# Add and gelu over 1024 x 4096 floats: another formula for the gelu, x in two loads, five adds moved to VectorE, another wait for the first store

## The chip, the cores and the metric

One core of a Trainium2 chip. The metric is the device time of one execution in microseconds (us), the median over runs of the same chip. A "span" is the time from the first to the last instruction in a profile, 1.4 to 1.7 us less than the device time. A ratio of two kernels is the mean time of one kernel's fast runs over the mean of the other's fast runs in the same rounds, so it is not quite the ratio of the medians quoted beside it.

## The reference

```python
x, y: 1024 x 4096 float32
z = x + y
out = 0.5 * z * (1 + tanh(sqrt(2/pi) * (z + 0.044715 * z**3)))
```

Each of the 128 partitions (rows of the on-chip memory) holds 32,768 elements (128 KB) of z. 33.55 MB come in, 16.78 MB go out.

## The kernel before

All transfers are issued by SyncE, an engine that computes nothing here, on one queue; VectorE, ScalarE and GpSimd compute. x, y and z lie in the on-chip memory SBUF, the tiles w in a second one, PSUM. z takes the place of x (one 128 KB row per partition); y goes through two buffers of 8192 columns, so y2 and y3 wait until y0 and y1 have been added. The columns are computed in 16 chunks of 2048, with two PSUM tiles w.

```python
loads = [8192, 8192, 8192, 8192]     # x and y, alternating: x0 y0 x1 y1 ...
FIRST = 9
stores = [16384, 10240, 6144]        # chunks 0-7, 8-12, 13-15
by_pool = set(range(1, C))           # adds on GpSimd: all but chunk 0
...
add(c):  z = z + y                                  # GpSimd (chunk 0: VectorE)
sq(c):   w = Square(root * z)                       # ScalarE, SBUF -> PSUM
stt(c):  w = (w + c1) * z                           # VectorE
sig(c):  w = Sigmoid(w)                             # ScalarE
mul(c):  z = w * z                                  # VectorE; chunk FIRST in two halves
...
store(0) also waits for the first half of mul(FIRST):
    reason="the stores join the queue when the last load is nearly done"
```

The moment at which the first store is issued is called the **join** below.

## Time and profile before

| | before |
|---|---|
| device time, median of 3 | 120.51 us (120.43 to 120.77) |
| span of the profiled run | 118.7 us |
| DMA engines busy | 98.8% of the span |
| VectorE / ScalarE / GpSimd busy | 73.7 / 61.0 / 69.6 us |
| first compute / join / last store issued | 21.85 / 77.34 / 106.77 us |

No compute engine is near full and the DMA engines are, so the reader should ask of each instruction only whether a transfer waits for it. The lines that carry this are shown in the prediction. One view adds to them, the longest entries of what SyncE's queue waited for (columns: who waited, for whom, us in total, times, longest):

```profile
SPq L139 <- DVE z L175: 46.2, 3, 17.8
SPq L135 <- POOL z L152: 31.4, 2, 18.1
SPq L135 <- DVE z L152: 21.6, 1, 21.6
```

SyncE waits most of the time for VectorE (stores) and GpSimd (y buffers). That looks like a bound by compute, but is not: while SyncE waits, the queue still holds transfers that it issued before.

### The profile page before, as it was taken

Reading aid. Unit: us, or ns where it says so; the run is one execution under the profiler, and the core shown is the slowest. Engines: PE = TensorE matmul, PEld = TensorE weight load, DVE = VectorE, ACT = ScalarE, POOL = GpSimd, SP = SyncE. Lnnn points to the kernel's source line nnn. Section 1 sums busy time; section 2 is a strip of 40 time slices with the busy share of each in tenths; the row PEclk is TensorE's granted clock in tenths of the full one; section 3 lists DMA queues with packets and bytes.
Section 4 is the critical chain, followed back from the end, with each engine's and each line's share of the span. In section 5 each row is a group of like instructions: output and inputs, shape, how many; then the busy total and the mean of one; then the engine's idle time right before and its main releaser. Section 6 shows DMA issues by size and latency. Waiting matters only on the chain.

```text
span 118.7 us, 172 instructions
## 1 busy us (share of the span) xinstructions
DVE 73.7 (62%) x35; ACT 61.0 (51%) x34; POOL 69.6 (59%) x19
## 2 busy tenths in 40 slices
DVE  0000000635799995739999968999994999990000
ACT  5000000063888965197698647888839779810000
POOL 0000000699996099999959999959999990000000
DMA  8989898989999898989999898998899889999896
GB/s 254 453 364 519 353 530 353 497 386 453 431 409 475 364 519 353 530 353 475 409 409 475 364 519 353 530 530 353 353 508 552 353 353 442 442 442 442 381 414 265
DMA packets 1584, 50.33 MB, mean 424 GB/s; under 512 B 176, under 2 KB 176, under 8 KB 176
## 3 DMA queue, kind: packets, MB, share of 16 engines
q1 hardware_dynamic: 1584, 50.33, 98.8%
HBM read 33.55 MB, written 16.78 MB: 424 GB/s over the span
## 4 chain that ended last, share of the span: by engine, by line
DMA 51%; POOL 26%; POOLq 4%; DVE 4%; DVEq 2%; ACT 2%; issue 0%; SPq 0%
DMA y<-in_y_dram 51%; POOL z L152 26%; POOLq L230 4%; DVE w L163 2%; DVEq L230 2%; DVE z L175 2%; ACT w L157 2%; SPq L128 0%; POOLq L152 0%
## 5 line engine op out<-in xcount | busy, mean ns | idle before, releaser
L152 POOL TENSOR_TENSOR z<-z,y 128x2048 f32<-128x2048 f32 x15 | 69.4, 4659 | 28.2 <-DMA y<-in_y_dram 28.2
L157 ACT ACTIVATE w<-z 128x2048 f32<-128x2048 f32 x16 | 30.1, 1882 | 37.6 <-DVE z L152 21.4
L163 DVE SCALAR_TENSOR_TENSOR w<-w,z 128x2048 f32<-128x2048 f32 x16 | 36.7, 2296 | 11.2 <-ACT w L157 11.0
L175 DVE TENSOR_TENSOR z<-w,z 128x2048 f32<-128x2048 f32 (+1 forms) x17 | 35.9, 2155 | 0.0
L168 ACT ACTIVATE w<-w 128x2048 f32<-128x2048 f32 x16 | 29.7, 1855 | 4.4 <-DVE w L163 4.3
L152 DVE TENSOR_TENSOR z<-z,y 128x2048 f32<-128x2048 f32 x1 | 2.3, 2293 | 20.5 <-DMA y<-in_y_dram 20.5
L215 ACT ACT_TABLE_LOAD x1 | 1.3, 1283 | 1.3 <-PEq L247 1.3
L214 DVE MEMSET one<- 128x1 f32 x1 | 0.1, 59 | 1.3 <-PEq L247 1.3
L247 POOL MEMSET const-float32-0.0<- 128x1 f32 x1 | 0.1, 99 | 0.2 <-issue 0.2
L215 ACT ACTIVATE one<-one 128x1 f32<-128x1 f32 x1 | 0.2, 203 | 0.0
L247 POOL MEMSET const-bfloat16-1.0<- 128x1 bf16 x1 | 0.1, 102 | 0.0
L247 POOL MEMSET const-uint8-127<- 128x1 uint8 x1 | 0.1, 102 | 0.0
L247 POOL MEMSET const-float32-1.0<- 128x1 f32 x1 | 0.1, 99 | 0.0
## 6 DMA issues: line engine op xcount, KB each, us to landing
z<-in_x_dram SPq DMA_DIRECT2D x4, 4096.0 KB, 31.3
y<-in_y_dram SPq DMA_DIRECT2D x4, 4096.0 KB, 22.2
out_dram<-z SPq DMA_DIRECT2D x1, 5120.0 KB, 15.8
out_dram<-z SPq DMA_DIRECT2D x1, 3072.0 KB, 11.9
out_dram<-z SPq DMA_DIRECT2D x1, 22.0
```

Source lines behind the costliest of these rows:

```text
L152: eng.tensor_add(out=zt[:, a:b], in0=zt[:, a:b], in1=yt[s][:, o : o + b - a])
L157: nc.scalar.activation(out=wt[c], in_=zt[:, a:b], func=act.Square, scale=root)
L163: nc.vector.scalar_tensor_tensor(out=wt[c], in0=wt[c], scalar=c1, in1=zt[:, a:b], op0=alu.add, op1=alu.mult)
L168: nc.scalar.activation(out=wt[c], in_=wt[c], func=act.Sigmoid)
L175: ins = nc.vector.tensor_mul(out=zt[:, a + o : a + o + n], in0=wt[c][:, o : o + n], in1=zt[:, a + o : a + o + n],)
L214: nc.vector.memset(one, 0.0)
L215: nc.scalar.activation(out=one, in_=one, func=act.Sigmoid)
L230: tc.compile()
L247: nc = _bacc.Bacc("TRN2", target_bir_lowering=False, num_devices=1)
```

## The change

The intent: gelu(z) = max(z, 0) + gelu(-|z|) needs one VectorE operation per chunk instead of two; VectorE can then take some of the adds from GpSimd; x in rows of 64 KB halves its packets.

```diff
-    loads = [8192, 8192, 8192, 8192]
-    FIRST = 9
+    xloads = [16384, 16384]
+    yloads = [8192, 8192, 8192, 8192]     # order: x0 y0 y1 x1 y2 y3
+    FIRST = 8
-    by_pool = set(range(1, C))
+    by_dve = {0: 0, 2: 0, 4: 2, 6: 4, 8: 8, 12: 10}   # add k on VectorE, ahead of end(by_dve[k])
...
-    sq:   w = Square(root * z)
-    stt:  w = (w + c1) * z
-    sig:  w = Sigmoid(w)
-    mul:  z = w * z
+    mag:  w = Abs(z)                          # ScalarE
+    gelu: w = Gelu_apprx_tanh(-1.0 * w)       # ScalarE
+    end:  z = max(z, 0) + w                   # VectorE, scalar_tensor_tensor
```

(The order on ScalarE becomes mag, gelu of one chunk after another, and the table loaded at the start is the gelu's.)

More of the change, by code (lines that the diff above doesn't have):

```diff
@@ L1 @@
 from contextlib import ExitStack
-import math
 import concourse.bass as bass
@@ L93 @@
     xv, yv, ov = (a.rearrange("(p n) d -> p (n d)", p=P) for a in (x, y, out))
-    c1 = 2.0 * math.sqrt(2.0 / math.pi)
-    root = math.sqrt(c1 * 0.044715)
     YS = 8192
@@ L108, in ranges @@
         return [(e - f, e) for e, f in zip(ends, sizes)]
-    lr, sr, cr = ranges(loads), ranges(stores), ranges([CH] * (TOT // CH))
+    xr, yr, sr, cr = (ranges(r) for r in (xloads, yloads, stores, [CH] * (TOT // CH)))
     C = len(cr)
-    by_pool = set(range(1, C))
+    by_dve = {0: 0, 2: 0, 4: 2, 6: 4, 8: 8, 12: 10}
     def over(rs, lo, hi):
@@ L123 @@
     zt = pool_sb.tile([P, TOT], fp32, tag="z", name="z")
-    yt, wt, muls = {}, {}, {}
+    yt, wt, ends = {}, {}, {}
     def load_x(i):
-        a, b = lr[i]
+        a, b = xr[i]
         nc.sync.dma_start(out=zt[:, a:b], in_=xv[:, a:b])
     def load_y(i):
-        a, b = lr[i]
+        a, b = yr[i]
         s, o = divmod(a, YS)
@@ L142, in store @@
                 ins.ins,
-                muls[FIRST].name,
+                ends[FIRST].name,
                 mybir.DependencyInfo(mybir.DependencyClass.Sync, mybir.DependencyReason.DATA),
@@ L150, in add, with mag, gelu, end @@
         s, o = divmod(a, YS)
-        eng = nc.gpsimd if c in by_pool else nc.vector
+        eng = nc.vector if c in by_dve else nc.gpsimd
         eng.tensor_add(out=zt[:, a:b], in0=zt[:, a:b], in1=yt[s][:, o : o + b - a])
-    def sq(c):
+    def mag(c):
         a, b = cr[c]
         wt[c] = pool_w.tile([P, CH], fp32, tag="w", name=f"w{c}")
+        nc.scalar.activation(out=wt[c], in_=zt[:, a:b], func=act.Abs)
+    def gelu(c):
         nc.scalar.activation(
-            out=wt[c], in_=zt[:, a:b], func=act.Square, scale=root
+            out=wt[c], in_=wt[c], func=act.Gelu_apprx_tanh, scale=-1.0
         )
-    def stt(c):
-        a, b = cr[c]
-        nc.vector.scalar_tensor_tensor(
-            out=wt[c], in0=wt[c], scalar=c1, in1=zt[:, a:b], op0=alu.add, op1=alu.mult
-        )
-    def sig(c):
-        nc.scalar.activation(out=wt[c], in_=wt[c], func=act.Sigmoid)
-    def mul(c):
+    def end(c):
         a, b = cr[c]
@@ L174, in mul @@
         for o in range(0, b - a, n):
-            ins = nc.vector.tensor_mul(
-                out=zt[:, a + o : a + o + n],
-                in0=wt[c][:, o : o + n],
-                in1=zt[:, a + o : a + o + n],
+            ins = nc.vector.scalar_tensor_tensor(
+                out=zt[:, a + o : a + o + n], in0=zt[:, a + o : a + o + n], scalar=0.0,
+                in1=wt[c][:, o : o + n], op0=alu.max, op1=alu.add,
             )
-            muls.setdefault(c, ins.ins)
+            ends.setdefault(c, ins.ins)
     sp = []
-    for i in range(len(loads)):
-        sp += [(load_x, i), (load_y, i)]
+    for i, (a, b) in enumerate(xr):
+        sp += [(load_x, i)] + [(load_y, j) for j, (c, _) in enumerate(yr) if a <= c < b]
     sp += [(store, i) for i in range(len(stores))]
-    pool = [(add, c) for c in range(C) if c in by_pool]
-    dve = [(add, c) for c in range(C) if c not in by_pool]
-    acts = [(sq, 0), (sq, 1)]
-    for c in range(0, C, 2):
-        dve += [(stt, c), (stt, c + 1), (mul, c), (mul, c + 1)]
-        acts += [(sig, c), (sig, c + 1)]
-        if c + 2 < C:
-            acts += [(sq, c + 2), (sq, c + 3)]
+    pool = [(add, c) for c in range(C) if c not in by_dve]
+    dve, acts = [], []
+    for c in range(C):
+        dve += [(add, k) for k in sorted(by_dve) if by_dve[k] == c] + [(end, c)]
+        acts += [(mag, c), (gelu, c)]
     needs = {
@@ L198 @@
         load_y: lambda i: [
-            (add, c)
-            for c in over(cr, lr[i][0] - 2 * YS, lr[i][0] - YS)
-            if lr[i][0] % YS == 0
-        ],
-        add: lambda c: [(f, i) for i in over(lr, *cr[c]) for f in (load_x, load_y)],
-        sq: lambda c: [(add, c)] + ([(mul, c - PS)] if c >= PS else []),
-        stt: lambda c: [(sq, c)],
-        sig: lambda c: [(stt, c)],
-        mul: lambda c: [(sig, c)],
-        store: lambda i: [(mul, c) for c in over(cr, *sr[i])] + [(mul, FIRST)],
+            (add, c) for c in over(cr, yr[i][0] - 2 * YS, yr[i][1] - 2 * YS)
+        ],
+        add: lambda c: [(load_x, i) for i in over(xr, *cr[c])]
+        + [(load_y, i) for i in over(yr, *cr[c])],
+        mag: lambda c: [(add, c)] + ([(end, c - PS)] if c >= PS else []),
+        gelu: lambda c: [(mag, c)],
+        end: lambda c: [(gelu, c)],
+        store: lambda i: [(end, c) for c in over(cr, *sr[i])] + [(end, FIRST)],
     }
@@ L214 @@
         nc.vector.memset(one, 0.0)
-        nc.scalar.activation(out=one, in_=one, func=act.Sigmoid)
+        nc.scalar.activation(out=one, in_=one, func=act.Gelu_apprx_tanh)
         while any(queues):
```

## The prediction

> **What bounds the kernel now.** I read the page first, then the timeline, the waits of the DMA queue, and the DMA view cut into stretches of 0.2 us. The page's queue and issue lines:
>
> ```profile
> span 118.7 us, 172 instructions
> q1 hardware_dynamic: 1584, 50.33, 98.8%
> HBM read 33.55 MB, written 16.78 MB: 424 GB/s over the span
> L152 POOL TENSOR_TENSOR z<-z,y 128x2048 f32<-128x2048 f32 x15 | 69.4, 4659 | 28.2 <-DMA y<-in_y_dram 28.2
> L157 ACT ACTIVATE w<-z 128x2048 f32<-128x2048 f32 x16 | 30.1, 1882 | 37.6 <-DVE z L152 21.4
> L175 DVE TENSOR_TENSOR z<-w,z 128x2048 f32<-128x2048 f32 (+1 forms) x17 | 35.9, 2155 | 0.0
> ```
>
> The 16 DMA engines are busy 98.8% of the span; no compute engine passes 62%. In the timeline GpSimd's first adds of the four y tiles start at 21.89, 41.31, 60.74 and 80.15: every 8.39 MB takes 19.4 us, 433 GB/s. Issue plus time to landing puts the stores' ends at 99.3 (77.34 + 22.0), 111.5 (95.66 + 15.8) and 118.7 (106.77 + 11.9), so the 8.39, 5.24 and 3.15 MB of stores run at 432 to 437 GB/s. One stream of 50.33 MB at 433 GB/s is 116.2 us; with some 2.4 us before the first and after the last byte it is the whole span. Compute matters only where it lets the stream run dry, and the one dangerous place is the join of the first store:
>
> ```profile
> 77.34 29.76 SPq L139 DMA_DIRECT2D out_dram<-z  x3
> ```
> ```profile
> 78.00:78.20 0.20, 0.20 (x1) 0.16 (x1) 0.20 (x1) 1.00 3.80 1638
> 78.20:78.40 0.20, 0.20 (x2) 0.00 (x0) 0.20 (x1) 1.00 1.90 819
> ...
> 79.20:79.40 0.20, 0.20 (x1) 0.20 (x1) 0.00 (x0) 1.00 5.32 2294
> 79.40:79.60 0.20, 0.20 (x1) 0.20 (x1) 0.00 (x0) 1.00 6.07 2622
> ...
> 81.60:81.80 0.20, 0.20 (x1) 0.20 (x1) 0.20 (x1) 1.00 5.29 2294
> 81.80:82.00 0.20, 0.20 (x1) 0.20 (x1) 0.20 (x1) 1.00 6.05 2621
> ```
>
> (last two columns: DMA share, GB/s.) Packets are recorded in bursts, one row on each of 16 engines. The last 32 KB rows of the loads are stamped near 78.2, the store's first 64 KB rows 1.2 us later, the next ones 2.4 us after those: exactly one row's time each, so nothing ran dry. The very first load, issued at 0.00, has its first stamps at 1.0 to 1.4, so I estimate 1.15 us from an issue to the first stamp. The store was issued at 77.34 and stamped at 79.4, that is 2.05 us. So it could come 0.9 us later, at about **78.2**, for nothing; later than that every us of delay is a us of the end. By the same sum the second store must be out one row slot after the first's eight rows, and the last one by about 109.7 (its first stamps, 110.8, less 1.15).
>
> **What the Trainium skill says.**
> 1. "DMA: Bandwidth & Descriptors", § Where 436 GB/s comes from: a fabric ceiling of 435 GB/s. The trace agrees, 433. There is nothing left to gain in rate: going from 433 to 435 on all of it would be 0.5 us.
> 2. "ScalarE: Activation LUTs", § What ACT_TABLE_LOAD costs: any function costs the same per element, 186 ns + 0.833 ns per element with immediates, 1892 ns at 2048. The trace has 1882 for Square and 1855 for Sigmoid, so Abs and the gelu should read the same, with one table load of 1283 ns as now.
> 3. "SBUF — State Buffer", § Who interferes with whom: VectorE and GpSimd share a port pair as an exclusive lock; a VectorE instruction with two SBUF inputs contends with a GpSimd one that reads SBUF, and whichever starts first blocks the other for the whole instruction; with one input in PSUM there is no contention. The trace agrees as far as it goes: VectorE's one add starts at 21.85 for 2.29 us, and the GpSimd add that starts at 21.89 takes 6.62 us where the minimum is 4.50; VectorE's work on PSUM tiles leaves GpSimd at 4.5. The other direction, VectorE behind a GpSimd add, does not occur in this trace.
>
> **The change part by part.**
> - *Formula.* Per chunk Square, (w+c)z, Sigmoid, w·z become Abs, gelu, max-plus-add. ScalarE stays at 2 per chunk, 16 × 3.74 = 60 us. VectorE loses 16 operations of 2.3 us (-36.7) and gains 5 adds of 2.29 (+11.5): 73.7 becomes about 49. GpSimd goes from 15 adds to 10: 69.6 becomes 45, plus any blocking. All of it lies beside the transfers: worth 0 by itself. The round trip ACT-DVE-ACT-DVE of a chunk becomes ACT-ACT-DVE.
> - *x in two loads.* 2 × 128 fewer packets; rows of 32 KB run at 432.5 GB/s (y landings), rows of 64 KB at 434 to 435 (first store), so 16.8 MB gain about 0.1 us. The first compute now waits for 12.58 MB instead of 8.39: 2.4 + 29.05 = 31.5 us, 9.7 later. Loads need no compute before y2, whose gate is the adds of chunks 0 to 3: 24 MB are queued by then, up to 59 us, and those adds end by about 45. y3's gate, adds 4 to 7, ends by 59, before y2 is through at 70. No gap.
> - *First store.* It needs half of chunk 8, whose y2 tile is now seventh of the eight quarter loads: it lands a quarter load (9.7 us) before the last at 80.0, at 70.3. Then VectorE add 2.29, Abs 1.88, gelu 1.86, half an end operation 1.21, four hand-overs of 0.05 to 0.1: 70.3 + 7.5 = **77.8**. That is 0.5 later than now and inside the 78.2. Effect 0.
> - *Tail.* After y2, ScalarE needs 8 × 3.8 us: 72.7 + 30.4 = 103, and the last end operation 105 to 108 with GpSimd's adds in the way, against a deadline of 109.7. Effect 0.
>
> Sum: 120.5 - 0.1, thus 120.4 if nothing blocks.
>
> **The rivals.**
> *A: hidden anyway* (above). For it: the stream at 98.8% and the deadlines just worked out.
> *B: the port lock becomes the wait.* The six VectorE adds meet GpSimd's. I laid the instructions out in time with the durations above, full blocking and first come first served: add 0 31.5 to 33.8, GpSimd add 1 to 38.3, VectorE add 2 to 40.6, GpSimd adds 3 and 5 to 49.6, VectorE add 4 to 51.9, end of chunk 2 at 54.2. ScalarE's chunk 4 waits for that (two PSUM buffers), then four chunks at 3.8 us: chunk 7's end operation runs from 69.4 to 71.7, still running when y2 lands at 70.3. GpSimd then takes the port with add 9 until 74.9, VectorE's add 8 runs to 77.2, and the join comes at 77.2 + 5.1 = **82.3**: 4.1 us past 78.2, so 120.5 + 4.1 = 124.6. Letting VectorE win ties gives the same. Against it: small shifts decide. If VectorE is free at 70.3 it wins, as it did at 21.85 against 21.89, and A holds; over plausible lags the late join came up in about three layouts of four. If VectorE is in fact never held by a running GpSimd add, also A.
> *C: faster by over 2%.* That means under 118.1 us, 2.4 us less, with 116.2 us of pure transfer at today's rate, 2.4 us of ends, and 1.8 us outside the span. Only a higher rate could do it, and the ceiling leaves 0.5.
>
> **Range and chances.** The mechanism of B is stated by the skill, but only half of it shows in the trace, and the placing of the adds looks made for a join just in time. I give B 0.42, A 0.54, C 0.04. My single number is the likelier branch with a little added for a late join: 120.8. The range reaches from a slightly better rate, 119.9, to B with 0.5 more, 125.2.
>
> **What would show it right or wrong.** Right: first compute at about 31.5; Abs and gelu near 1.88 and 1.86; y2's first use at 70.3, first store issued at 77.8 (before 78.2), DMA share still near 98.8% and rows evenly spaced through 80. B shows as VectorE adds (or the idle time ahead of them) of up to 4.5 us more, a store issued near 82 and a hole of 4 us in the bursts between 78 and 84. Wrong in another way: rows of 64 KB that run at another rate, a second table load, or a hole at y2, y3 or a later store.

## The result, and the profile after

120.30 us median (120.20 to 120.41, 4 runs) against 120.62 (120.43 to 120.77, 4 runs): ratio 0.9974, 95% interval 0.9955 to 0.9994. It is the same time within 2%, 0.3 us shorter at best. A repeat gave 120.23 against 120.37, ratio 0.9988, interval 0.9975 to 1.0002.

The page of the kernel after, with the lines that answer to those of before:

```profile
span 118.8 us, 160 instructions
DVE 59.8 (50%) x24; ACT 60.8 (51%) x34; POOL 55.5 (47%) x14
q1 hardware_dynamic: 1296, 50.33, 98.5%
L149 POOL TENSOR_TENSOR z<-z,y 128x2048 f32<-128x2048 f32 x10 | 55.3, 5560 | 45.9 <-DMA y<-in_y_dram 45.9
L154 ACT ACTIVATE w<-z 128x2048 f32<-128x2048 f32 x16 | 30.1, 1880 | 42.8 <-DVE z L149 36.3
L149 DVE TENSOR_TENSOR z<-z,y 128x2048 f32<-128x2048 f32 x6 | 24.0, 4009 | 30.6 <-DMA y<-in_y_dram 30.6
L157 ACT ACTIVATE w<-w 128x2048 f32<-128x2048 f32 x16 | 29.8, 1862 | 0.5
```

VectorE and GpSimd each lost 14 us of busy time, the packets fell from 1584 to 1296, and the span did not move: all of it lay beside the transfers. Two means stand out. A GpSimd add averages 5560 ns where 4.5 us is its time alone, and a VectorE add 4009 ns where it is 2.29. They hold each other up, at the port that point 3 of the prediction describes. The list of the adds' durations (ns, min/median/max) says the same:

```profile
L149 POOL TENSOR_TENSOR z<-z,y x10: 4509/5550/6634, 31.7 to 97.1; 128x2048 f32<-128x2048 f32 x10
L149 DVE TENSOR_TENSOR z<-z,y x6: 2280/3636/6593, 31.7 to 83.3; 128x2048 f32<-128x2048 f32 x6
```

A blocked instruction is recorded as busy, so the wait for the port does not appear as idle time. The timeline around the join (start, duration, engine, line, operation):

```profile
67.91 2.29 DVE L166 SCALAR_TENSOR_TENSOR z<-z,w 128x2048 f32<-128x2048 f32 x1 [1.46 <-ACT w L157]
70.48 2.29 DVE L149 TENSOR_TENSOR z<-z,y 128x2048 f32<-128x2048 f32 x1 [0.29 <-DMA y<-in_y_dram]
70.53 6.62 POOL L149 TENSOR_TENSOR z<-z,y 128x2048 f32<-128x2048 f32 x1 [14.56 <-DMA y<-in_y_dram]
72.81 1.88 ACT L154 ACTIVATE w<-z 128x2048 f32<-128x2048 f32 x1 [5.00 <-DVE z L149]
76.62 2.35 DVE L166 SCALAR_TENSOR_TENSOR z<-z,w 128x1024 f32<-128x1024 f32 x2 [3.84 <-ACT w L157]
77.86 30.28 SPq L136 DMA_DIRECT2D out_dram<-z  x3
```

VectorE ended chunk 7 at 70.20 and was idle for 0.29 us when y2 landed. It started its add 0.05 us ahead of GpSimd, ran it undisturbed while GpSimd's took 6.62 us, and the join came at 77.86.

### The profile page after: what moved, and what is told of

It is laid out like the page before. It is cut to its first block, busy times and chain, and to the rows that moved or that the text cites. A ratio compares the mean times of both kernels' runs of the same rounds, so it can differ in the third digit from the quotient of the medians.

```text
span 118.8 us, 160 instructions
## 1 busy us (share of the span) xinstructions
DVE 59.8 (50%) x24; ACT 60.8 (51%) x34; POOL 55.5 (47%) x14
## 2 busy tenths in 40 slices
DMA packets 1296, 50.33 MB, mean 424 GB/s; under 512 B 144, under 2 KB 144, under 8 KB 144
## 3 DMA queue, kind: packets, MB, share of 16 engines
q1 hardware_dynamic: 1296, 50.33, 98.5%
## 4 chain that ended last, share of the span: by engine, by line
DMA 48%; POOL 33%; POOLq 4%; ACT 3%; DVE 2%; issue 0%; SPq 0%; DVEq 0%
DMA y<-in_y_dram 48%; POOL z L149 33%; POOLq L215 4%; DVE z L166 2%; ACT w L154 2%; ACT w L157 2%; SPq L125 0%; POOLq L149 0%; DVEq L166 0%
## 5 line engine op out<-in xcount | busy, mean ns | idle before, releaser
L149 POOL TENSOR_TENSOR z<-z,y 128x2048 f32<-128x2048 f32 x10 | 55.3, 5560 | 45.9 <-DMA y<-in_y_dram 45.9
L166 DVE SCALAR_TENSOR_TENSOR z<-z,w 128x2048 f32<-128x2048 f32 (+1 forms) x17 | 36.3, 2156 | 16.0 <-ACT w L157 16.0
L149 DVE TENSOR_TENSOR z<-z,y 128x2048 f32<-128x2048 f32 x6 | 24.0, 4009 | 30.6 <-DMA y<-in_y_dram 30.6
```

Of the source, the lines that this page charges most:

```text
L149: eng.tensor_add(out=zt[:, a:b], in0=zt[:, a:b], in1=yt[s][:, o : o + b - a])
L166: ins = nc.vector.scalar_tensor_tensor(out=zt[:, a + o : a + o + n], in0=zt[:, a + o : a + o + n], scalar=0.0, in1=wt[c][:, o : o + n], op ...
```

## The experiments

Theory A: the time is one unbroken stream of transfers, and compute matters only through the moments at which stores join. Rival B: the port that VectorE and GpSimd share can hold up chunk 8's add and make the join late. A smaller question is where the 0.3 us come from. Three groups of runs follow, each against the kernel before on the same chip; every output was correct. The join is that of the profiled execution. The diffs are cut to their core.

| run | change to the kernel after | join, us | median, us | before, us | ratio (95%) |
|---|---|---|---|---|---|
| after_again | none | 78.03 | 120.23 | 120.37 | 0.9988 (0.9975 to 1.0002) |
| e6_store_early | first store waits for chunk 7 only | 70.10 | 120.98 | 120.37 | 1.0048 (1.0035 to 1.0061) |
| e1_x_in_four | x in four loads | 72.50 | 121.10 | 120.37 | 1.0059 (1.0047 to 1.0072) |
| e2_formula_alone | also old adds, FIRST = 9 | 74.84 | 121.18 | 120.37 | 1.0067 (1.0054 to 1.008) |
| e3_whole_chunk | first store waits for all of chunk 8 | 78.93 | 120.72 | 120.37 | 1.0033 (1.0016 to 1.0049) |
| e5_adds_on_gpsimd | old adds | 80.22 | 122.99 | 120.37 | 1.0211 (1.0196 to 1.0225) |
| e9_chunk_nine | FIRST = 9 | 82.27 | 123.99 | 120.37 | 1.0295 (1.0282 to 1.0308) |
| e4_nudge | VectorE busy 0.48 us before add 8 | 78.02 | 120.31 | 120.37 | 0.999 (0.9977 to 1.0003) |
| e10_nudge_more | three such writes before add 8 | 82.37 | 124.07 | 120.43 | 1.0297 (1.027 to 1.0324) |
| e1b_x_in_four_timed | x in four loads, join set | 77.31 | 120.21 | 120.43 | 0.9976 (0.9959 to 0.9994) |
| e2b_formula_timed | formula alone, join set | 77.88 | 120.44 | 120.43 | 1.0003 (0.9981 to 1.0026) |
| e8_loads_alone | (kernel before) x in two loads | 87.14 | 128.99 | 120.43 | 1.0703 (1.068 to 1.0727) |

### One part at a time, and an early join

The kernel after, once more, unchanged:

> The changed kernel once more, to see whether its 0.3 us over the kernel before are real. Theory A (everything hidden behind the transfers; only rows and fixed parts differ): 120.2 to 120.5, ratio 0.996 to 0.999. Rival (noise): ratio 1.000.

It is 0.14 us ahead, and the interval of its ratio includes 1.

```diff
-    xloads = [16384, 16384]
+    xloads = [8192, 8192, 8192, 8192]
```

> The changed kernel with x in four loads of 32 KB rows again. If the long rows bring the 0.3 us, this reads 120.5 to 120.6, like the kernel before. If they bring only my estimate of 0.1 us or nothing (the rest from elsewhere), 120.3 to 120.4. First compute back at about 21.9, the store's join near 68 to 70, behind queued loads, harmless.

```diff
+    xloads = [8192, 8192, 8192, 8192]
+    by_dve = {0: 0}
+    FIRST = 9
```

> The new formula alone: loads, adds (all but chunk 0 on GpSimd) and the store's wait as in the kernel before. Theory: ScalarE and VectorE work lies beside the transfers, so taking a third of VectorE's work away changes nothing: 120.3 to 120.6, VectorE busy down from 73.7 to about 39. Rival: the formula itself is what saves 0.3 us: 120.3, with e1 also 120.3.

```diff
-    FIRST = 8;  parts = 2 if c == FIRST else 1
+    FIRST = 7;  parts = 1
```

> The changed kernel with the first store's wait on chunk 8 taken away: it needs only chunks 0 to 7 and joins near 70.3 instead of 77.9. Theory (one queue in order, loads before it): unchanged, 120.3. Rival (stores that come early mix with the last two y loads and hold them up): y3 lands later than 80, the tail moves; up to 10 us of y3 delay would bring the last store past its deadline and cost some us.

All three were slower by 0.75 to 0.95 us than the kernel after. The expectations of the first two missed this; e6's rival, stores that hold up the last loads, is what came, with under 1 us in place of up to 10. (e1's join was also missed: 72.5, not 68 to 70.) What the three share is a join before the last load is nearly done: at 70.1, 72.5 and 74.8. The DMA view in stretches of 0.2 us (last two columns: busy share of the 16 DMA engines, GB/s) shows where it is lost. A packet is counted whole in the stretch in which it starts, so shares go above 1. The next to last burst of load rows in the kernel after:

```profile
76.40:76.60 0.20, 0.00 (x0) 0.18 (x1) 0.20 (x1) 1.00 0.38 164
76.60:76.80 0.20, 0.18 (x1) 0.00 (x0) 0.20 (x1) 1.00 2.67 1147
76.80:77.00 0.20, 0.20 (x1) 0.00 (x0) 0.20 (x1) 1.00 2.28 983
...
77.20:77.40 0.20, 0.20 (x1) 0.20 (x1) 0.20 (x1) 1.00 0.76 328
```

and in e6_store_early:

```profile
76.60:76.80 0.20, 0.20 (x1) 0.00 (x0) 0.20 (x1) 1.00 3.22 819
76.80:77.00 0.20, 0.20 (x1) 0.00 (x0) 0.20 (x2) 1.00 2.83 819
77.00:77.20 0.20, 0.20 (x1) 0.14 (x1) 0.20 (x2) 1.00 3.24 983
...
78.20:78.40 0.20, 0.20 (x1) 0.20 (x1) 0.20 (x1) 1.00 0.44 164
78.40:78.60 0.20, 0.20 (x1) 0.20 (x1) 0.20 (x1) 1.00 0.50 164
78.60:78.80 0.20, 0.19 (x1) 0.20 (x1) 0.20 (x1) 1.00 3.49 1311
78.80:79.00 0.20, 0.00 (x0) 0.17 (x2) 0.20 (x1) 1.00 1.70 655
79.00:79.20 0.20, 0.00 (x0) 0.20 (x1) 0.20 (x1) 1.00 0.88 328
```

The reader should divide share by bytes. In the kernel after the shares of this burst sum to 6.09, times 0.2 us is 1.22 us per row, for 0.52 MB, one 32 KB row on each engine. In the early kernel the same 0.52 MB carry 9.29 x 0.2 = 1.86 us, and the next 0.52 MB, the last of the loads, 7.01 x 0.2 = 1.40 us: 3.26 instead of 2.44 us for the last two rows, 0.8 us more. In e2_formula_alone the two take 1.64 + 1.58 us, again 0.8 more. In e1_x_in_four they take 1.89 + 1.23 us, 0.7 more. So the loss sits where the loads end, and it does not grow with earliness. That a store which joins 4.5 us or more before the loads would have ended (79.3) slows the last load rows is what the runs show; by what mechanism, they don't.

To tell the parts from the join, two of the runs were repeated with the join put back. For x in four loads the store waits for all of chunk 9; for the formula alone it waits for three idle writes on VectorE after chunk 9:

```diff
+    FIRST = 9;  parts = 1                                   # x in four loads
...
+    dve: ..., end(9), pad, pad, pad, end(10), ...           # formula alone
+    pad: memset of 128 x 512;  store(0) waits for the last pad
```

> The changed kernel with x in four loads, and the first store waiting for all of chunk 9 so that it joins near 77.3 and not at 72.5. If the 0.7 us of e1 came from the early join: 120.3 to 120.4, span about 118.8. If they came from the short rows: still 121.1.

> The formula alone (loads and adds of the kernel before), with three idle writes on VectorE after chunk 9 that set the first store's join to about 77.4 instead of 74.8. If an early join is what cost 0.8 us: 120.3 to 120.4. If the formula itself costs it: 121.2.

Both came back, to 120.21 and 120.44 us. So the early join cost the 0.7 to 0.9 us, not the rows and not the formula. And the long rows of x bring nothing that can be measured: 120.21 with short ones, 120.23 and 120.30 with long ones.

```diff
     kernel before
-    loads = [8192, 8192, 8192, 8192]         # x and y alternating
+    xloads = [16384, 16384]; yloads = [8192, 8192, 8192, 8192]
```

> The kernel before with x in two loads and nothing else changed. Its y2 then lands at 70.4 instead of 60.6, the two chunks 8 and 9 go through GpSimd adds (79.5), Square, the VectorE step, Sigmoid (85.6) and half a product: join near 87.2, 8.7 us past 78.5: 129.1. Rival (loads hidden in any order): 120.4.

128.99 us with a join at 87.14. The loads of the change, alone, cost 8.5 us, since y2 lands a whole quarter of x later. The other parts of the change pay this back through a shorter chain from y2 to the join: the store waits for half of chunk 8 and no longer of chunk 9 (worth 3.7 us in e9_chunk_nine below), and chunk 8's add is on VectorE (e5_adds_on_gpsimd).

### A late join

```diff
-        parts = 2 if c == FIRST else 1
+        parts = 1
```

> The changed kernel with the first store waiting for all of chunk 8: it joins near 79.0 instead of 77.9. By the prediction's deadline of 78.2 this is 0.8 us too late: 121.0. Rival (the deadline is later, the last loads end at about 80): 120.3.

```diff
-    FIRST = 8
+    FIRST = 9
```

> The changed kernel with the first store waiting for half of chunk 9, join near 82.3, adds and port untouched. A late join alone then costs 82.3 - 78.2 = 4.1 us: 124.4, the same as the nudge if the nudge's cost is all in the join. If the late join is made good elsewhere: less.

Joins at 78.93 and 82.27 cost 0.47 and 3.74 us over 120.25 (between the two medians of the kernel after, 120.23 and 120.30). Taken off the joins, that is a deadline of 78.46 and 78.53; e8_loads_alone gives 87.14 - 8.74 = 78.40 (78.58 if its delay is counted from the kernel before, 120.43). Three runs over 8 us of delay agree: after about 78.5 a late join is paid one for one. In e9_chunk_nine the queue is empty when the store comes:

```profile
78.20:78.40 0.20, 0.20 (x1) 0.20 (x1) 0.20 (x1) 1.00 1.52 655
78.40:78.60 0.20, 0.20 (x1) 0.20 (x1) 0.20 (x1) 1.00 0.38 164
78.60:83.00 4.40, 2.26 (x3) 3.66 (x3) 4.40 (x2) 1.00 0.00 0
83.00:83.20 0.20, 0.20 (x1) 0.20 (x1) 0.20 (x1) 1.00 9.21 3932
83.20:83.40 0.20, 0.20 (x2) 0.20 (x1) 0.20 (x1) 1.00 3.07 1311
```

The third line is the hole: 4.4 us in which no packet starts. The stamps are starts, since these first 64 KB rows last 2.4 us each and are stamped 0.85 us after the issue at 82.27. The last load rows, 1.2 us each, still run into the hole: by the packets' own records they end at 79.3 on average over the 16 engines, and the store's rows start at 83.2, so 3.9 us are idle. In all five runs with a late join the first stamp comes 0.84 to 0.85 us after the issue and the mean one 0.9, not the 1.15 that the prediction had taken from the first load of the program. Then 79.3 - 0.9 = 78.4 is the deadline, close to the 78.5 that the times give.

```diff
-    by_dve = {0: 0, 2: 0, 4: 2, 6: 4, 8: 8, 12: 10}
+    by_dve = {0: 0}
```

> The changed kernel with all adds but the first on GpSimd, as in the kernel before. Chunk 8's add then ends at 75.0 instead of 72.8, the store joins near 80.1: 1.9 us late; GpSimd ends its last add near 106.5, the last store joins at about 112.7 against a deadline of 109.7 + 1.9: 1.1 more. 123.3. Rival (adds on GpSimd hidden): 120.3.

122.99 us. The join at 80.22 accounts for 1.7 us; the last store, issued at 112.6 against 110.8 + 1.7 - 0.85 = 111.65, for 0.95. Together 120.25 + 2.65 = 122.9. So with x in two loads the moved adds are needed, twice: at the join and at the end.

### The shared port

```diff
     dve: ..., end(7),
+    pad,                       # memset of 128 x 512 on VectorE
     add(8), end(8), ...
```

> The changed kernel with one idle write of 512 elements (about 0.6 us) on VectorE ahead of its add of chunk 8, so that VectorE is busy when y2 lands. Rival B of the prediction: GpSimd's add 9 takes the port at about 70.5 until 75.0, VectorE's add 8 ends at 77.3, the store joins at about 82.3, hole of about 4 us, 124.4. If VectorE could start its add beside a running GpSimd add: join 78.3, 120.4.

It missed: the write took 0.48 us, from 70.30, and VectorE still went first. The timeline:

```profile
70.30 0.48 DVE L162 MEMSET idle<- 128x512 f32 x1
70.56 6.73 POOL L149 TENSOR_TENSOR z<-z,y 128x2048 f32<-128x2048 f32 x1 [14.54 <-DMA y<-in_y_dram]
70.70 2.23 DVE L149 TENSOR_TENSOR z<-z,y 128x2048 f32<-128x2048 f32 x1
```

GpSimd's record begins at 70.56, ahead of VectorE's at 70.70, and yet VectorE's add ran its full speed; the GpSimd add took 6.73 us, so it was GpSimd that waited. So the order in which the two records start does not tell which of the two has the port. With three writes:

```diff
     dve: ..., end(7),
+    pad, pad, pad,
     add(8), end(8), ...
```

> The nudge again with three idle writes (about 1.4 us; the one of 0.48 us left VectorE free at 70.7 and it still went first, although GpSimd's record begins at 70.56). VectorE free near 71.7. Rival B of the prediction: GpSimd's add 9 holds the port until about 75.1, the add of chunk 8 ends near 77.3, the store joins near 82.4. With the deadline of 78.5 that the two late joins gave: 120.3 + 3.9 = 124.2. If a running GpSimd add doesn't hold VectorE here: join 79.0, 120.8.

```profile
70.64 4.50 POOL L149 TENSOR_TENSOR z<-z,y 128x2048 f32<-128x2048 f32 x1 [14.55 <-DMA y<-in_y_dram]
71.03 0.48 DVE L162 MEMSET idle<- 128x512 f32 x1 [0.17 <-DVE idle L162]
71.69 0.48 DVE L162 MEMSET idle<- 128x512 f32 x1 [0.17 <-DVE idle L162]
72.09 5.19 DVE L149 TENSOR_TENSOR z<-z,y 128x2048 f32<-128x2048 f32 x1
77.32 1.88 ACT L154 ACTIVATE w<-z 128x2048 f32<-128x2048 f32 x1 [9.38 <-DVE z L149]
82.37 0.35 SPq L136 DMA_DIRECT2D out_dram<-z  x1
```

Now VectorE's add takes 5.19 us instead of 2.29: it ends at 77.28, so its own 2.29 us began at 75.0, when GpSimd's add, begun at 70.64 with 4.5 us of work, was over. The join is at 82.37 and the time 124.07 us, to 0.1 us what an equally late join costs without any port in it (e9_chunk_nine, 123.99). Three writes of 0.48 us on an engine that is busy half of the time cost 3.8 us, through a lock and then a queue run dry.

No run beat the kernel after by more than the spread; the three best (e1b_x_in_four_timed, after_again, e4_nudge) lie between 120.21 and 120.31. With the stream unbroken there is nothing left to hide.

## Why the prediction was right

Branch A of it was what happened, and A's own sum, 120.4, is what to hold against the 120.3. The single number, 120.8, was a mixture that neither branch says, and the range, 119.9 to 125.2, took in both. That A held was in part luck: the prediction's layout gave a late join in three cases of four, and on the chip VectorE came free only 0.28 us ahead of y2's first use (e4_nudge and e10_nudge_more show how little more would have turned it). By its steps:

- **The bound.** A stream of 433 GB/s that compute must not interrupt: confirmed. VectorE's busy time fell by 14 us and the span stayed at 118.8. The late joins were paid one for one.
- **The formula.** Abs 1.88 and gelu 1.86 us, one table load of 1.28 us: as said (its 1892 ns is an estimate from the formula that it cites). VectorE's busy time was 59.8 and not 49, GpSimd's 55.5 and not 45: the adds' blocked time counts as busy. Alone, with the join in place, the formula is worth 0 (e2b_formula_timed).
- **x in two loads.** First compute at 31.70 against 31.5. y2 and y3 were issued at 44.92 and 58.18, where the prediction had 45 and 59, and left no gap. (The "24 MB" queued by then are 25.2 MB; nothing hangs on it.) The gain of 0.1 us did not show (e1b_x_in_four_timed).
- **The join.** y2's first use at 70.48 against 70.3, join at 77.86 against 77.8. The deadline was a little off: 78.5, not 78.2, since the start-up latency of the first load was the wrong measure for a later one. And "could come 0.9 us later for nothing" was only half of the story: the prediction never asked what an earlier join does, and it costs 0.8 us. The free window has its end at 78.5; its beginning lies between 74.84 and 77.31.
- **The tail.** Last end operation over at 107.78, inside the predicted 105 to 108 and the deadline. e5_adds_on_gpsimd, which broke that deadline, paid for it.
- **Rival B.** Its mechanism is real, in both directions, and its size was right (124.07 against 124.6). What failed is the layout that put chunk 7's end at 71.7. There GpSimd's add 5 and VectorE's add 4 both became ready near 45.1, and GpSimd took the port. On the chip VectorE's add 4 went first, at 44.82; its add 6 was held up instead:

```profile
44.82 2.28 DVE L149 TENSOR_TENSOR z<-z,y 128x2048 f32<-128x2048 f32 x1
52.50 5.62 DVE L149 TENSOR_TENSOR z<-z,y 128x2048 f32<-128x2048 f32 x1
```

  The tie alone does not explain it: the prediction says that ties to VectorE give the same late join, and redone so with its durations (an estimate) chunk 7 ends near 70.9, still after 70.3. What turned the sign were tenths. The steps of that chain were a little shorter than laid out (VectorE's operations follow each other in 2.20 us, not 2.29; two chunks on ScalarE took 7.46 us, not 7.6), and y2 was used 0.2 us later. So chunk 7 ended at 70.20, 0.28 us ahead of y2's first use. Nor is "first come first served" exact to such tenths: in e4_nudge VectorE was busy until 70.78, 0.2 us after GpSimd's record had begun, and still went first. The prediction saw that small shifts decide and gave B 0.42; its layout was not good to tenths of a microsecond.

Where the 0.1 to 0.3 us come from by which the kernel after leads can be narrowed down. One of its two measurements and the run with x in four loads show a lead (0.9974, 0.9976); the other and e4_nudge do not exclude that there is none (0.9988, 0.999), and the formula alone shows none (1.0003). The spans do not differ, so the lead lies outside the span. Device time less span is 1.44 to 1.54 us in every run of the kernel after and its variants with adds moved to VectorE, and 1.60 to 1.70 us in every run of the kernels with all adds but the first on GpSimd (the kernel before, e2, e2b, e5, e8). Some 0.15 us thus go with the moved adds and not with the transfers; why, no run shows.

## What to carry to other kernels

When one stream of transfers fills the span, measure each store's window instead of counting busy time: here the join was free from about 77.3 to 78.0, cost 0.8 us when at 74.8 or earlier and one for one after 78.5. A change that touches order, like larger loads, shifts those windows by whole transfers and must be judged together with the work that hits them. Engines that share a port make a schedule depend on who is ready a few tenths of a microsecond earlier: there, delay one side on purpose and see how much margin is left; here it lay between one and three idle writes.

## What the Trainium skill lacked or had wrong

- "DMA: Bandwidth & Descriptors" says nothing of what a store costs that is queued behind loads which are still running: three kernels whose store was issued 4.5 to 9 us before the loads would have ended took 0.75 to 0.95 us more, and the last two load rows took 3.1 to 3.3 us instead of 2.4. With the store issued 1.3 to 2 us before that end there was no such cost.
- The same page, § Where 436 GB/s comes from, says that for transfers between HBM, the main memory, and SBUF the HBM side (about 358 GB/s) binds. With this one core in use, 433 GB/s were sustained, near the fabric's figure. The sentence lacks its condition, which the page gives elsewhere, under its table of measured rates (425 GB/s for 16 MB): about 358 is a core's share when both cores of the pair stream.
- "SBUF — State Buffer", § Who interferes with whom, has the exclusive lock right in both directions (GpSimd 6.63 us behind VectorE, VectorE 5.19 behind GpSimd). It lacks two things that one needs to read a profile: a blocked instruction is recorded as busy, and the instruction whose record starts first need not hold the port (GpSimd's record at 70.56, VectorE's at 70.70, and VectorE went first).
- "DMA: Bandwidth & Descriptors", § Latency and other measured facts, gives about 600 ns to the first byte of a DMA issued from SyncE, without saying from where to where it counts. From the start of the issue's record to the first stamp of the packets it was 0.85 us here for a store on an empty queue, 1.0 us for the first load of the program (0.9 and 1.2 on average over the 16 engines).
